# Merge and output projection of a hybrid decoder layer: block products with resident weights in place of a loop over groups with reloaded weights

## The chip, the cores and the metric

The kernel runs on one core of a Trainium2 chip. The metric is the device time of one execution in microseconds (us). Its engines run side by side, each through its own list of instructions in order: TensorE (PE) multiplies matrices, with its loads of the stationary operand shown apart as PEld; VectorE (DVE), ScalarE (ACT) and GpSimd (POOL) work on elements; SyncE (SP) issues the transfers between the memory on the chip and DRAM.

## The reference

The layer works on 2048 prompt tokens and on 32 sample tokens (8 sequences of 4). Three token mixers give `o_a` (512 channels, stick-breaking attention), `o_b` (512 channels, pooling) and `o_c` (1024 channels, gated linear attention). What the change touches is the end:

```
gates  = sigmoid(mg).reshape(B, T, 3, 1024)
merged = gates[:, :, 0] * (o_a @ w_pa) + gates[:, :, 1] * (o_b @ w_pb) + gates[:, :, 2] * (o_c @ w_pc)
y      = x + merged @ w_o
```

`w_pa` and `w_pb` are 512 x 1024, `w_pc` and `w_o` are 1024 x 1024. All inputs are float32, and the result is wanted in nearly that precision.

## The kernel before, in words

Every float32 matrix is held as two parts, hi (a rounded copy, cast by ACT) and lo (the rest, a subtraction on DVE or POOL). A product of two matrices then is three matmuls (hi x hi, hi x lo, lo x hi), issued by `mm3` (L114), 128 channels deep each. So whatever is multiplied first has to be cast and subtracted.

The program has three phases. Phase a (projections, attention, pooling) and phase b (gated linear attention) write the mixers' outputs to scratch in DRAM (`od`, 16 blocks of 128 channels for each of the 4 groups of 512 tokens; group 0 carries the 32 sample tokens as well and is 544 wide) and the gates (`gd`, 24 blocks). Phase c is the merge and the output projection. `phase_c` goes through the groups in the order 1, 2, 3, 0. For each one:

- it loads the 16 blocks of `od` as 8 tiles `oraw` (L1563), casts them on ACT (L1567) and subtracts on DVE (L1568);
- in each of 4 steps `dp` of 256 output channels it takes the weights of `w_pa`, `w_pb` and `w_pc`, multiplies (512 tokens wide, into PSUM banks `z`), applies the gates on DVE (L1597, L1600, L1602) and adds the branches on POOL (L1604); ACT and POOL split the merged block into `mh` and `ml` (L1607, L1608);
- in each of 4 more steps it takes the weights of `w_o` and multiplies with tokens stationary and 256 weight columns moving, into banks `pj`; DVE adds `x` (L1625), and the result is stored (L1626). For group 0 the sample tokens follow (L254, L255, L1632, L1633).

The weights come through `take`: raw tiles `wr` are loaded some steps ahead (L157), cast on ACT (L173) and subtracted on DVE and POOL in turn (L175). All 12 MB of weights go through that once for each of the 4 groups. The order of instructions on each engine is set at build time by a scheduler that puts later work forward where its own costs say that it fits; the chip then follows it to the letter. So phase c's first loads and casts stand inside the end of phase b, whose last steps are the normalisation of the last head (L1405, L283 to L288, L1414), eight transposes (L119), two copies `ocT` (L1447) and their stores to `od` (L1452).

Of the kernel before, what the change touches and what calls it, by code (L numbers as in the profile page):

```python
# [17 lines left out]
P = 128  # L18
# [58 lines left out]
def hybrid_step(ctx, tc, x_prompt, x_sample, cache_k, cache_v, state_pool, state_gla, page_table, norm_g, w_in,  # L77
# [21 lines left out]
    wp = ctx.enter_context(tc.tile_pool(name="wp", bufs=1))  # L99
# [122 lines left out]
    def plan_c(g):  # L222
        us = []
        for d0 in range(0, D, 256):
            us += [[(wpa[:, :, d0:d0 + 256], 256)], [(wpb[:, :, d0:d0 + 256], 256)]] + halves(wpc, [(d0, 256)])
        for d0 in range(0, D, 256):
            us += halves(wo, [(d0, 256)])
        return [(seg, "s", "gv") for seg in us]

# [67 lines left out]
    od = [[dtile([P, ncols(g)], f"od{g}_{k}") for k in range(16)] for g in range(NG)]  # L297
    gd = [[dtile([P, ncols(g)], f"gd{g}_{k}") for k in range(24)] for g in range(NG)]
# [6 lines left out]
    hp = ctx.enter_context(tc.tile_pool(name="hp", bufs=1))  # L305
# [9 lines left out]
    def phase_a(ctx):  # L315
# [298 lines left out]
        def v_step(st):  # L614
# [10 lines left out]
            if c == 0 and pr == 1:  # L625
                h = hd_.h
                if h % 2 == 0:
                    hd_.pair[0] = ap_.tile([P, TG], F32, name="oT", bufs=OTB)
                oT = hd_.pair[0]
                r = slice(64 * (h % 2), 64 * (h % 2) + 64)  # L630
                ro = slice(64 - 64 * (h % 2), 128 - 64 * (h % 2))
                nc.scalar.copy(oT[r], hd_.acc[ro])
                nc.vector.tensor_tensor(oT[r], oT[r], hd_.acc[r], op=add)
                nc.gpsimd.tensor_tensor(oT[r], oT[r], hd_.sg[r, :TG], op=mul)
                if h % 2 == 1:
                    nc.sync.dma_start(od[g][h // 2][:, :TG], oT)
# [57 lines left out]
        def pool_group(g, p, hT):  # L694
# [72 lines left out]
            nc.sync.dma_start(od[g][4 + p], ob[:, :n])  # L767
# [8 lines left out]
        def gate_unit(g, u, hT):  # L776
# [3 lines left out]
            for j, c0, m in ([(j, *sp) for sp in spans for j in range(2)] if u == gates_a(g) - 1 else  # L780
# [6 lines left out]
                if c0 + m == ncols(g):  # L787
                    nc.sync.dma_start(gd[g][u * 2 + j], gts[j][:, :ncols(g)])

        def gate_last(g, hT):  # L790
# [4 lines left out]
            for c0 in range(0, TG, 256):  # L795
                for u, w, gt in zip(us, ws, gts):
                    for j in range(2):
# [5 lines left out]
                        if c0:  # L803
                            nc.sync.dma_start(gd[g][u * 2 + j], gt[j][:, :TG])
# [110 lines left out]
    def sample_attn(ctx, cst):  # L915
# [67 lines left out]
        for bt in range(2):  # L983
# [68 lines left out]
            for c in range(4):  # L1052
                nc.sync.dma_start(od[0][c][:, TG + bt * 16:TG + (bt + 1) * 16], og[:, c, :])


    def phase_b(ctx):
# [157 lines left out]
        def proj_gate(g, hh, hT):  # L1214
            w = win_unit([(OFF_MG + (8 + hh) * 256, 256)])
            for j in range(2):
# [3 lines left out]
                nc.sync.dma_start(gd[g][(8 + hh) * 2 + j], gt[:, :ncols(g)])  # L1220

        def mix_head(g, hh, st, later=None):
# [218 lines left out]
            def finish():  # L1441
                for j in range(2):
# [9 lines left out]
                    nc.sync.dma_start(od[g][8 + hh * 2 + j], oT[:, :n])  # L1452
# [90 lines left out]
    def phase_c(ctx):  # L1543
        mq = ctx.enter_context(tc.tile_pool(name="mrq", bufs=1, reuse_waits="tile"))
        on = ctx.enter_context(tc.tile_pool(name="on", bufs=1, reuse_waits="tile"))
        mp = ctx.enter_context(tc.tile_pool(name="mrg", bufs=1, reuse_waits="tile"))
        oe = ctx.enter_context(tc.tile_pool(name="oe", bufs=1, reuse_waits="tile"))
        o1 = ctx.enter_context(tc.tile_pool(name="o1", bufs=1, reuse_waits="tile"))
        N = TG + TS

        def o_tiles(gi, k2):
            if k2 < 4 and gi % 2:
                return [HT[x][:, k2 * 2:k2 * 2 + 2, :] for x in range(2)]
            return [(on if k2 > 1 else o1).tile([P, 2, N], F32R, name=f"o{x}{k2}") for x in "hl"]

        for gi, g in enumerate((1, 2, 3, 0)):
            n = ncols(g)
            cols = ((0, 256), (256, 288)) if g == 0 else ((0, TG),)
            oh, ol = [], []
            for k2 in range(8):  # L1560
                raw = oe.tile([P, 2, N], F32, name="oraw", bufs=3)
                for i in range(2):
                    nc.sync.dma_start(raw[:, i, :n], od[g][k2 * 2 + i])  # L1563
                th, tl = o_tiles(gi, k2)
                oh.append(th)
                ol.append(tl)
                nc.scalar.copy(oh[k2][:, :, :n], raw[:, :, :n])  # L1567
                nc.vector.tensor_tensor(ol[k2][:, :, :n], raw[:, :, :n], f32(oh[k2])[:, :, :n], op=sub)  # L1568
            mh = mq.tile([P, NC, TG], F32R, name="mh")
            ml = mq.tile([P, NC, TG], F32R, name="ml")  # L1570
            mS = mq.tile([P, NC, 2 * TS], F32R, name="mS")
            for dp in range(4):
                d0 = dp * 256
                ms = [mp.tile([P, N], F32, name="m", bufs=2) for _ in range(2)]
                for br in range(3):
                    gts = []
                    for j in range(2):
                        gt = mp.tile([P, N], F32, name="gt", bufs=4)
                        nc.sync.dma_start(gt[:, :n], gd[g][br * 8 + dp * 2 + j])
                        gts.append(gt)  # L1580
                    if br < 2:
                        src = (wpa, wpb)[br]
                        wh, wl = take([(src[:, :, d0:d0 + 256], 256)])
                        wsl = [(wh[0][:, c], wl[0][:, c], br * 4 + c) for c in range(4)]
                    else:
                        wh, wl = take(*halves(wpc, [(d0, 256)]))
                        wsl = [(wh[c // 4][:, c % 4], wl[c // 4][:, c % 4], 8 + c) for c in range(8)]
                    for j in range(2):
                        js = slice(j * P, (j + 1) * P)
                        for c0, m in cols:  # L1590
                            cs = slice(c0, c0 + m)
                            ps = bank("z")
                            drain(mm3(ps[:, :m], [((a[:, js], b_[:, js]),
                                                   (oh[k // 2][:, k % 2, cs], ol[k // 2][:, k % 2, cs]))
                                                  for a, b_, k in wsl]))
                            if br == 0:
                                nc.vector.tensor_tensor(ms[j][:, cs], ps[:, :m], gts[j][:, cs], op=mul)  # L1597
                            else:
                                if br == 1:
                                    nc.vector.tensor_tensor(gts[j][:, cs], ps[:, :m], gts[j][:, cs], op=mul)  # L1600
                                else:
                                    nc.vector.scalar_tensor_tensor(gts[j][:, cs], gts[j][:, cs], 1.0, ps[:, :m],  # L1602
                                                                   op0=add, op1=mul)
                                nc.gpsimd.tensor_tensor(ms[j][:, cs], ms[j][:, cs], gts[j][:, cs], op=add)  # L1604
                for j in range(2):
                    c = dp * 2 + j
                    nc.scalar.copy(mh[:, c, :], ms[j][:, :TG])  # L1607
                    nc.gpsimd.tensor_tensor(ml[:, c, :], ms[j][:, :TG], f32(mh)[:, c, :], op=sub)  # L1608
                    if g == 0:
                        nc.scalar.copy(mS[:, c, :TS], ms[j][:, TG:])  # L1610
                        nc.gpsimd.tensor_tensor(mS[:, c, TS:], ms[j][:, TG:], f32(mS)[:, c, :TS], op=sub)
            for dp in range(4):
                d0 = dp * 256
                w = take(*halves(wo, [(d0, 256)]))
                pss = [bank("pj") for _ in range(2)]
                for cs in ((0, 6), (6, NC)) if dp == 0 else ((0, NC),):
                    for i in range(4):
                        proj_part(w, (mh, ml), i * P, P, pss[i // 2][:, i % 2 * 256:(i % 2 + 1) * 256], *cs,
                                  i % 2 == 0 or dp > 0)
                for pr in range(2):  # L1620
                    ps = pss[pr]
                    t0 = g * TG + pr * 256
                    xt = mq.tile([P, 2, 256], F32, name="xt", bufs=2)
                    nc.sync.dma_start(xt, xp[t0:t0 + 256, d0:d0 + 256].rearrange("(i p) n -> p i n", p=P))
                    nc.vector.tensor_tensor(xt, xt, ps.rearrange("p (i n) -> p i n", n=256), op=add)  # L1625
                    nc.sync.dma_start(yp[t0:t0 + 256, d0:d0 + 256].rearrange("(i p) n -> p i n", p=P), xt)  # L1626
                if g == 0:
                    xy = mq.tile([P, 2, 256], F32, name="xt", bufs=2)[:TS]
                    xt, yt = xy[:, 0], xy[:, 1]
                    nc.sync.dma_start(xt, xs[:, d0:d0 + 256])  # L1630
                    drain(proj_smp(w, mS, yt))
                    nc.vector.tensor_tensor(xt, xt, yt, op=add)  # L1632
# [53 lines left out]
```

## Time and profile before

| | |
|---|---|
| time, median of 3 runs | 3106.36 us (3098.63 to 3110.66) |
| the profiled execution: time / span | 3105.42 us / 3103.7 us |
| mean granted TensorE clock | 0.985 of full speed |
| share of the span that is busy: PE, DVE, ACT, POOL | 96%, 59%, 41%, 38% |
| traffic to and from DRAM over the span | 202 GB/s |
| phase c: first matmul to last instruction | 2540.99 to 3103.7 us |

The span runs from the first to the last instruction; the execution's own time lies 1.7 us above it. A granted clock of 1.00 is 2.4 GHz, half of it 1.2 GHz. Busy shares are means over a program of very different stages, so for a change in phase c the rows of phase c count.

### The profile page before, as it was taken

How to read it: one execution, taken by the hardware profiler on the slowest of the kernel's cores; microseconds unless marked ns; L12 is line 12 of the kernel's file. 1: busy time of each engine (PE TensorE's matmuls, PEld its weight loads, DVE VectorE, ACT ScalarE, POOL GpSimd, SP SyncE). 2: the span in 40 equal slices, each digit the busy share in tenths (PEclk: the TensorE clock that was granted, in tenths of full speed). 3: DMA queues.
4: the chain of work that ended last, by engine and by line, in shares of the span. 5: the costliest groups of instructions: out<-in, count | busy, mean ns of one | idle time of the engine just before them, and what ended most of it. 6: DMA issues, size and time to landing. Idle time of an engine off the chain costs nothing.

```text
span 3103.7 us, 55924 instructions
## 1 busy us (share of the span) xinstructions
PE 2983.7 (96%) x21874; PEld 2628.6 (85%) x21874; DVE 1843.9 (59%) x3776; ACT 1284.5 (41%) x2411; POOL 1183.4 (38%) x1161
## 2 busy tenths in 40 slices
PE   7999999999999999999989999999999989999999
PEld 7889987789878888777779988888778778988999
DVE  7776455656766778888745655545455564343332
ACT  2333334453554545665644433334334443232221
POOL 4556232314232434332224333333434436344452
PEclk9999999999999999999999999999999989999999
DMA  8867764556645764445565676564464456766553
GB/s 290 285 228 249 290 219 169 193 204 236 213 170 202 243 239 144 155 144 171 174 216 200 230 247 222 178 221 175 158 215 166 170 175 212 226 207 190 175 160 111
DMA packets 303037, 626.24 MB, mean 202 GB/s; under 512 B 26353, under 2 KB 188493, under 8 KB 265645
## 3 DMA queue, kind: packets, MB, share of 16 engines
q1 hardware_dynamic: 297652, 605.87, 57.7%
q0 software_dynamic: 5120, 16.78, 1.7%
q8 instruction: 173, 2.83, 0.4%
q14 instruction: 92, 0.75, 0.1%
HBM read 452.47 MB, written 170.28 MB: 201 GB/s over the span
## 4 chain that ended last, share of the span: by engine, by line
PE 42%; DVE 5%; ACT 3%; DMA 2%; issue 1%; SPq 1%; POOL 0%; ACTq 0%; DVEq 0%; POOLq 0%
PE pj L114 24%; PE z L114 13%; PE at L114 2%; PE acc L114 1%; DMA hTl<-hd 1%; PE z L119 1%; PE at L119 1%; DVE lv L1117 0%; PE acc L119 0%; DVE lv L1120 0%; DVE gate L1414 0%; DVE scx L1359 0%; ACT L1148 0%; DMA oraw<-od 0%; ACT lv L1119 0%
## 5 line engine op out<-in xcount | busy, mean ns | idle before, releaser
L114 PE MATMUL pj<-hTh,w 128*128 128x512 f32 (+2 forms) x3648 | 1055.8, 355 | 7.2 <-DVE ut L758 5.3
L114 PEld LDWEIGHTS pj<-hTh,w 128*128 128x128 f32 x3648 | 645.1, 189 | 111.9 <-issue 27.5
L114 PE MATMUL pj<-w,hTh 128*128 128x256 f32 (+1 forms) x3680 | 707.2, 292 | 13.0 <-DMA hTh<-hd 6.8
L114 PE MATMUL pj<-hTl,w 128*128 128x512 f32 (+2 forms) x1824 | 632.0, 346 | 0.0
L114 PEld LDWEIGHTS pj<-w,hTh 128*128 128x128 f32 (+1 forms) x3680 | 576.3, 191 | 31.2 <-issue 9.6
L114 PE MATMUL pj<-w,hTl 128*128 128x256 f32 (+1 forms) x1840 | 526.1, 286 | 7.9 <-DVE hTl L422 4.1
L585 POOL TENSOR_TENSOR be<-be,om 128x512 f32<-128x512 f32 (+1 forms) x160 | 167.8, 1049 | 556.4 <-DVE om L580 518.6
L114 PEld LDWEIGHTS pj<-hTl,w 128*128 128x128 f32 x1824 | 345.7, 190 | 26.7 <-issue 1.2
L175 POOL TENSOR_TENSOR w<-wr,w 128x1024 fp32r<-128x1024 f32 x104 | 255.6, 2458 | 284.5 <-ACT w L173 174.5
L114 PEld LDWEIGHTS pj<-w,hTl 128*128 128x128 f32 (+1 forms) x1840 | 352.7, 192 | 9.3 <-DVE hTl L422 4.5
L580 DVE TENSOR_TENSOR_SCAN om<-om,car 128x512 f32<-128x512 f32 x192 | 267.2, 1393 | 80.6 <-ACT om L572 80.4
L571 ACT ACTIVATE be<-z,bB 128x512 f32<-128x512 f32 (+2 forms) x320 | 200.3, 626 | 212.1 <-DVE z L568 136.8
L611 ACT CAST ah<-at 128x512 fp32r<-128x512 f32 (+2 forms) x352 | 160.8, 493 | 259.3 <-PE at L119 190.4
L612 DVE TENSOR_TENSOR al<-at,ah 128x512 fp32r<-128x512 f32 (+2 forms) x352 | 188.8, 563 | 118.5 <-ACT ah L611 117.7
L114 PE MATMUL z<-oh,w 128*128 128x512 f32 (+2 forms) x896 | 251.1, 365 | 0.0
L173 ACT CAST w<-wr 128x1024 fp32r<-128x1024 f32 x122 | 128.0, 1049 | 256.3 <-PE z L114 126.5
L572 ACT ACTIVATE om<-z,nbB 128x512 f32<-128x512 f32 (+2 forms) x320 | 200.4, 626 | 0.0
L114 PEld LDWEIGHTS z<-oh,w 128*128 128x128 f32 x896 | 161.4, 189 | 28.8
L114 PE MATMUL pj<-w,mh 128*128 128x256 f32 x1024 | 184.5, 283 | 0.6 <-ACT mh L1607 0.6
L119 PE MATMUL at<-ident,be 128*128 128x128 f32 x1088 | 148.0, 274 | 16.4 <-DVE qT L519 9.0
L114 PE MATMUL z<-ol,w 128*128 128x512 f32 (+2 forms) x448 | 163.6, 366 | 0.0
L114 PEld LDWEIGHTS pj<-w,mh 128*128 128x128 f32 x1024 | 159.6, 192 | 1.1 <-ACT mh L1607 0.8
(509 smaller groups left out, 5291.4 us busy)
## 6 DMA issues: line engine op xcount, KB each, us to landing
w<-wk SPq DMA_DIRECT2D x216, 1024.0 KB
wk<-w SPq DMA_DIRECT2D x72, 1024.0 KB
wr<-in_w_in_dram SPq DMA_DIRECT2D x56, 512.0 KB
gt<-gd SPq DMA_DIRECT2D x72, 256.0 KB
wr<-in_w_pc_dram SPq DMA_DIRECT2D x32, 512.0 KB
wr<-in_w_o_dram SPq DMA_DIRECT2D x32, 512.0 KB
gd<-gt SPq DMA_DIRECT2D x62, 256.0 KB
x<-in_x_prompt_dram SPq DMA_DIRECT2D x26, 512.0 KB
```

Of the source, the lines that this page charges most:

```text
L114: i = nc.tensor.matmul(*a, **k)
L119: i = nc.tensor.transpose(*a, **k)
L173: nc.scalar.copy(wh, raw)
L175: (nc.vector if el[count[0] % len(el)] == "v" else nc.gpsimd).tensor_tensor(wl, raw, f32(wh), op=sub)
L571: nc.scalar.activation(be[:, :w], z[:, :w], AF.Sigmoid, bias=bB[:, h:h + 1], scale=0.125)
L572: nc.scalar.activation(om[:, :w], z[:, :w], AF.Sigmoid, bias=nbB[:, h:h + 1], scale=-0.125)
L580: nc.vector.tensor_tensor_scan(ov, ov, ov, init, op0=mul, op1=ALU.min)
L585: (nc.vector if i % 2 == 0 else nc.gpsimd).tensor_tensor(be[:, :w], be[:, :w], om[:, 1:w + 1], op=mul)
L611: nc.scalar.copy(ah[:, jr, tr_], pv[:, jr, tr_])
L612: nc.vector.tensor_tensor(al[:, jr, tr_], pv[:, jr, tr_], f32(ah)[:, jr, tr_], op=sub)
```

## The change

Phase c is written anew as three stages, each of which goes through all groups with one set of weights, loaded and split once.

Stage 1 is the two small branches, plain: units of (group, branch) for the groups 1, 2, 0, 3, with `w_pa` and `w_pb` resident as 8 tiles `opw`. Each unit is as many matmuls as before, of the same shapes. The gated sum of the two goes to DRAM (`md[0]`).

Stage 2 is the third branch for the groups 0 to 3, as a Strassen-Winograd product: both matrices are cut into 2 x 2 blocks, and sums and differences of blocks are formed so that 7 block products do in place of 8. `left` and `right` form these operands on DVE (4 adds of 1024 columns for a group, and 4 for each half of the weights). The 7 weight operands are 14 tiles, resident for all groups. The products accumulate in three chains of PSUM banks (`PROD`: x, y, x, z, x, z, x). The adds that put the quadrants together, the gate, and the sum from `md[0]` are on DVE (`branch_evict`); the result goes to `md[1]`. Tokens are 256 wide (272 in group 0) where they were 512 (256 and 288).

Stage 3 is the output projection for the groups 1, 2, 3, 0 in the same way, with weights 512 columns wide as the moving side, where they were 256. The operands of `w_o` are formed during the last group of stage 2. The sample tokens take 32 matmuls beside the last group.

POOL keeps 7 of the weights' subtractions; all other work of that kind is DVE's. The pools of phases a and b are closed ahead of phase c (`front.close()`), and `od` and `gd` become one DRAM tile for each group. The rest of the diff in phases a and b follows from this, and the order of their instructions is nearly the one of before. The core of the diff:

```diff
-        for gi, g in enumerate((1, 2, 3, 0)):
...
-                for br in range(3):
...
-                        wh, wl = take(*halves(wpc, [(d0, 256)]))
...
-                w = take(*halves(wo, [(d0, 256)]))
...
+        def split(hi, lo, raw, eng=nc.vector):
+            nc.scalar.copy(hi, raw)
+            eng.tensor_tensor(lo, raw, f32(hi), op=sub)
+
+        def left(load, new, put):
+            a11 = load(0, 0)
+            yield put(a11)
+            a12 = load(0, 1)
+            yield put(a12)
+            a21, a22 = load(1, 0), load(1, 1)
+            s1, w = new()
+            nc.vector.tensor_tensor(s1, a21, a22, op=add)
+            nc.vector.tensor_tensor(a21, a11, a21, op=sub)
+            nc.vector.tensor_tensor(a11, s1, a11, op=sub)
+            yield put(a11)
+            yield put(s1)
+            yield put(a21)
+            nc.vector.tensor_tensor(a12, a12, a11, op=sub)
+            yield put(a12)
+            yield put(a22)
...
+        def put_w(raw):
+            t = ww.tile([P, 2, 2, TG], F32R, name="opw", bufs=14)
+            turn[0] += 1
+            split(t[:, 0], t[:, 1], raw, nc.gpsimd if turn[0] % 2 and turn[0] <= 14 else nc.vector)
+            return t
...
+        def product(ch, start, ws, acts, branch):
+            w = ch.w
+            ks = [(kp, kk) for kp in range(len(ws)) for kk in range(2)]
+            for m in range(4 if branch else 2):
...
+                    for x, y in ((0, 0), (0, 1), (1, 0)):
+                        n += 1
+                        mm(out, lhsT=L[x], rhs=R[y], start=start and m % ch.per == 0 and n == 1,
...
+        def run(dst, acts, w, branch, evict, each=None):
+            chains = {}
+            for i, kind in enumerate(PROD):
+                while len(dst[i]) < dst.need:
+                    go(1)
+                a = acts(i)
+                if i in (0, 1, 3):
+                    chains[kind] = Chain("x" if kind == "x" else "z", w)
+                product(chains[kind], i in (0, 1, 3), dst[i], a, branch)
+                evict(i, chains[kind])
...
+        def branch_evict(g):
...
+                gt = tile_g()[:, :, :w]
+                nc.sync.dma_start(gt, gd[g][:, 16 + fi * 4:16 + fi * 4 + 4, cs])
+                m = tile_g()[:, :, :w]
+                nc.sync.dma_start(m, md[0][g][:, rows, cs])
...
+                    for ps, sb in ch.parts(v):
+                        nc.vector.tensor_tensor(sb, ps, sb, op=add)
+                    nc.vector.scalar_tensor_tensor(v, gt, 1.0, v, op0=add, op1=mul)
...
+                nc.vector.tensor_tensor(v, v, m, op=add)
+                nc.sync.dma_start(md[1][g][:, rows, cs], v)
...
+            units = [(g, br) for g in (1, 2, 0, 3) for br in range(2)]
...
+        acts = feed([operand(od[g], 8, 4, ncols(g) // 2, right) for g in range(NG)], 1)
+        for g in range(NG):
+            if g == NG - 1:
+                plan_w([weights(wo, 4, kp, right) for kp in range(2)], wq, two)
+            run(wc, acts, ncols(g) // 2, True, branch_evict(g), (lambda i: go(1)) if g in (0, NG - 1) else None)
+        ORD = (1, 2, 3, 0)
...
+        acts = feed([operand(md[1][g], 0, 4, 256, left) for g in ORD], 1)
```

Three places of the order show what moved. The first is ScalarE where phase c begins. Before, these were its rows (`oh` is the hi part of phase c's first operands, `w` of its first weights, `ocT` the last copy of phase b):

```order
L1567 CAST oh_29855<-oraw 128x2x512
L1369 CAST Sh<-S_22340 128x256
L1405 ACTIVATE junk,gss<-at 128x256
L1567 CAST oh_29862<-oraw 128x2x512
L173 CAST w_29917<-wr 128x1024
L1369 CAST Sh<-S_22340 128x256
L1405 ACTIVATE junk,gss<-at 128x256
L1184 ACTIVATE gate<-pj 128x512
L173 CAST w_29920<-wr 128x1024
L1405 ACTIVATE junk,gss<-at 128x256 x2
L1447 COPY ocT<-z 128x512 x2
```

Now the same place reads (lines from here on are those of the changed kernel; `opw` is a weight operand, `opa` an activation operand; L1399 is the former L1405, L1441 the former L1447):

```order
L1363 CAST Sh<-S_22196 128x256
L1399 ACTIVATE junk,gss<-at 128x256
L1178 ACTIVATE gate<-pj 128x512
L1399 ACTIVATE junk,gss<-at 128x256 x2
L1441 COPY ocT<-z 128x512 x2
L1553 CAST opw<-rw 128x1024 x5
L1553 CAST opa_29738<-ra_29736 128x2x512
L1553 CAST opa_29743<-ra_29741 128x2x512
```

Four casts of phase c stood ahead of the copies `ocT`; now none does, and five casts of weights stand between the copies and the first operand.

The second place is VectorE where stage 1 passes into stage 2 (L1799 applies a gate, L1803 adds the branches, L1554 is the subtraction of a split, L1580 to L1587 form operands):

```order
L1799 TENSOR_TENSOR gt_31009<-z,gt_31009 128x512
L1554 TENSOR_TENSOR opw<-rw,opw 128x1024
L1799 TENSOR_TENSOR gt_31009<-x,gt_31009 128x512
L1554 TENSOR_TENSOR opw<-rw,opw 128x1024
L1803 TENSOR_TENSOR gt_31009<-gt_31009,gt_30877 128x2x512
L1554 TENSOR_TENSOR opa<-ra,opa 128x544 x4
L1580 TENSOR_TENSOR ra<-ra 128x1088
```

Before, VectorE passed from the small branches into the third one with nothing between the gates but a weight's subtraction:

```order
L1600 TENSOR_TENSOR gt<-z,gt 128x512 x2
L1602 SCALAR_TENSOR_TENSOR gt<-gt,z 128x512
L175 TENSOR_TENSOR w_30217<-wr,w_30217 128x1024
L1602 SCALAR_TENSOR_TENSOR gt<-gt,z 128x512
L1597 TENSOR_TENSOR m<-z,gt 128x512 x2
```

The operands' subtractions now stand behind the last gate and the last add of stage 1 and behind two weight tiles.

The third place is VectorE where stage 2 passes into stage 3 (L1731 and L1732 are the last evictions of stage 2, L1563 to L1569 form the operands of stage 3's first group, L1840 and L1846 add to `x`):

```order
L1564 TENSOR_TENSOR ra<-ra 128x4x256
L1587 TENSOR_TENSOR rw<-rw 128x1024
L1554 TENSOR_TENSOR opw<-rw,opw 128x1024
L1840 TENSOR_TENSOR gt<-x,gt 128x512
L1554 TENSOR_TENSOR opw<-rw,opw 128x1024
L1840 TENSOR_TENSOR gt<-x,gt 128x512
L1732 TENSOR_TENSOR tmp<-tmp,gt 128x4x256
L1554 TENSOR_TENSOR opw<-rw,opw 128x1024
L1732 TENSOR_TENSOR gt<-gt 128x4x256
L1554 TENSOR_TENSOR opw<-rw,opw 128x1024
L1565 TENSOR_TENSOR ra<-ra 128x4x256
L1554 TENSOR_TENSOR opw<-rw,opw 128x1024
```

Before, where it passed from the merge into the projection, it stood so:

```order
L1602 SCALAR_TENSOR_TENSOR gt<-gt,z 128x512
L1568 TENSOR_TENSOR ol_31013<-oraw,oh_31012 128x2x512
L1568 TENSOR_TENSOR ol_31020<-oraw,oh_31019 128x2x512
L1568 TENSOR_TENSOR ol_32094<-oraw,oh_32093 128x2x512
L1568 TENSOR_TENSOR ol_32101<-oraw,oh_32100 128x2x512
L175 TENSOR_TENSOR w_30627<-wr,w_30627 128x1024
L1568 TENSOR_TENSOR ol_32108<-oraw,oh_32107 128x2x512
L1625 TENSOR_TENSOR xt<-xt,pj 128x512 x2
```

Then it prepared the next group's operands there; now five of the 14 weight tiles of `w_o` and the first operands of stage 3 stand between the evictions of both stages.

## Rows read from the trace of the kernel before

**Rows 1.** The page's part on busy time: us, share of the span, instructions.

```profile
PE 2983.7 (96%) x21874; PEld 2628.6 (85%) x21874; DVE 1843.9 (59%) x3776; ACT 1284.5 (41%) x2411; POOL 1183.4 (38%) x1161
```

**Rows 2.** Waits of PE in phase c, 2548 to 3100 us: total, times, longest.

```profile
PE pj L114 <- ACT mh L1607: 0.6, 1, 0.6
PE pj L114 <- POOL ml L1608: 0.4, 1, 0.4
```

**Rows 3.** The chain that ended last: start, us, engine, work, instructions.

```profile
2522.82 4.10 DMA oraw<-od
2538.83 2.50 PE z L119 x8
2541.33 90.82 PE z L114 x384
2632.16 46.07 PE pj L114 x384
...
2678.23 89.17 PE z L114 x384
...
3047.00 53.02 PE pj L114 x445
```

**Rows 4.** Stretches: us, busy time (instructions) of each engine, granted clock, DMA.

```profile
2530.00:2550.00 20.00, 14.07 (x62) 11.24 (x61) 13.75 (x27) 8.62 (x16) 3.59 (x2) 0.74 0.66 210
...
2700.00:2750.00 50.00, 50.00 (x217) 40.39 (x216) 15.37 (x19) 12.57 (x14) 28.98 (x19) 1.00 0.55 164
...
2900.00:2950.00 50.00, 50.00 (x402) 49.22 (x401) 18.71 (x17) 14.59 (x15) 16.26 (x8) 1.00 0.57 179
```

**Rows 5.** Timeline of ACT at the start of phase c: start, us, work [idle before].

```profile
2527.00 1.05 ACT L1567 CAST oh<-oraw 128x1024 fp32r<-128x1024 f32 x1 [2.67 <-DMA oraw<-od]
...
2540.52 0.59 ACT L1447 COPY ocT<-z 128x512 f32<-128x512 f32 x1 [5.82 <-PE z L119]
2541.37 0.59 ACT L1447 COPY ocT<-z 128x512 f32<-128x512 f32 x1 [0.27 <-PE z L119]
2541.85 2.94 ACT L1567 CAST oh<-oraw 128x1024 fp32r<-128x1024 f32 x3
```

**Rows 6.** Timeline of SP's issues there.

```profile
2522.16 10.04 SPq L1563 DMA_DIRECT2D oraw<-od  x10
...
2541.13 1.17 SPq L1452 DMA_DIRECT2D od<-ocT  x2
```

**Rows 7.** Timeline of PE there.

```profile
2538.83 2.50 PE L119 MATMUL z<-ident,gate 128*128 128x128 f32 x8 [4.71 <-DVE gate L1414]
2540.99 0.78 PE L114 MATMUL z<-oh,w 128*128 128x512 f32 x1
...
2542.84 0.63 PE L114 MATMUL z<-ol,w 128*128 128x512 f32 x1
2543.26 1.05 PE L114 MATMUL z<-oh,w 128*128 128x512 f32 x2
...
2544.55 0.82 PE L114 MATMUL z<-oh,w 128*128 128x512 f32 x2
```

**Rows 8.** DVE and ACT: groups by shape, phase c (busy us, mean ns).

```profile
L1602 DVE SCALAR_TENSOR_TENSOR gt<-gt,z 128x512 f32<-128x512 f32 x24 | 16.4, 684 | 53.3 <-PE z L114 53.3
...
L173 ACT CAST w<-wr 128x1024 fp32r<-128x1024 f32 x92 | 96.6, 1050 | 236.6 <-PE z L114 126.5 <-PE pj L114 95.2 <-DMA wr<-in_w_pa_dram 5.9
```

**Rows 9.** DVE's subtractions, whole run or phase c: min/median/max ns, first and last start.

```profile
L175 DVE TENSOR_TENSOR w<-wr,w x46: 1212/1226/2614, 2549.7 to 3073.6; 128x1024 fp32r<-128x1024 f32 x46
...
L1317 DVE TENSOR_TENSOR qsl<-qs,qsh x16: 665/688/740, 1664.4 to 2518.3; 128x512 fp32r<-128x512 f32 x16
```

**Rows 10.** The end: timeline, last matmuls and last store.

```profile
3098.02 1.99 PE L114 MATMUL pj<-w,mS 128*64 128x256 f32 x16
...
3101.32 0.34 SPq L1633 DMA_DIRECT2D out_dram<-xt  x1
```

**Rows 11.** Transfers from 2540 to 3104 us: GB/s in 40 slices, and the whole.

```profile
GB/s 256 321 297 198 141 191 188 331 246 192 217 180 137 188 151 168 266 305 171 245 202 186 133 185 177 158 176 197 179 227 92 199 127 186 161 62 115 158 96 65
DMA packets 87240, 105.30 MB, mean 187 GB/s; under 512 B 5024, under 2 KB 67744, under 8 KB 87200
```

More of the change, by code (lines that the diff above doesn't have):

```diff
@@ L1556, in phase_c @@
-        for gi, g in enumerate((1, 2, 3, 0)):
[L1557 to L1574, printed above, removed]
-                for br in range(3):
-                    gts = []
-                    for j in range(2):
[L1578 to L1584, printed above, removed]
-                    else:
-                        wh, wl = take(*halves(wpc, [(d0, 256)]))
[L1587 to L1613, printed above, removed]
-                w = take(*halves(wo, [(d0, 256)]))
[L1615 to L1632, printed above, removed]
-                    nc.sync.dma_start(ys[:, d0:d0 + 256], xt)
@@ new lines, in put_w, with weights, load @@
+        def put_w(raw):
[3 more added lines that the diff above has]
+            return t
+        def weights(src, half, kp, form):
+            def load(i, j):
+                k, f = (j, i) if form is left else (i, j)
+                raw = raw_w()
+                c = k * half + kp * 2
+                nc.sync.dma_start(raw, src[:, c:c + 2, f * TG:(f + 1) * TG])
+                return raw
+            return form(load, lambda: (raw_w(), 0), put_w)
@@ new lines, in operand, with view, load, put @@
+        def operand(src, c0, half, w, form):
+            def view():
+                return raw_a()[:, :half, :w]
+            def load(i, j):
+                k, t = (i, j) if form is right else (j, i)
+                raw = view()
+                c = c0 + k * half
+                nc.sync.dma_start(raw, src[:, c:c + half, t * w:(t + 1) * w])
+                return raw
+            def put(raw):
+                got = []
+                for kp in range(half // 2):
+                    t = op_.tile([P, 2, 2, HW], F32R, name="opa", bufs=4)
+                    split(t[:, 0, :, :w], t[:, 1, :, :w], raw[:, kp * 2:kp * 2 + 2, :])
+                    got.append(t)
+                return got
+            return form(load, lambda: (view(), 0), put)
@@ new lines, in phase_c, with go, plan_w, step @@
+        steps = []
+        def go(n):
+            for _ in range(n):
+                if steps:
+                    steps.pop(0)()
+        def plan_w(gens, dst, order):
+            for i, k in order:
+                def step(g=gens[k], d=dst[i]):
+                    d.append(next(g))
+                steps.append(step)
+        def run(dst, acts, w, branch, evict, each=None):
[8 more added lines that the diff above has]
+                evict(i, chains[kind])
+                if each is not None:
+                    each(i)
@@ new lines, in feed, with get, tile_t, tile_g @@
+        def feed(gens, depth):
+            it = (v for g in gens for v in g)
+            ahead_ = []
+            def get(_):
+                while len(ahead_) < depth + 1:
+                    v = next(it, None)
+                    if v is None:
+                        break
+                    ahead_.append(v)
+                return ahead_.pop(0)
+            return get
+        def tile_t():
+            return tt.tile([P, 4, HW], F32, name="tmp", bufs=3)
+        def tile_g():
+            return gg.tile([P, 4, HW], F32, name="gt", bufs=5)
```

241 lines of the change are left out of this document (210 added, 31 removed).

## The prediction

> **What bounds the kernel now.** I read the page's busy times first [rows 1]: PE has work in 96% of the span, the others far less, so I look for waits of PE in the part that changes. From 2548 us to the end it waited twice, for 1.0 us together [rows 2]. The chain that ended last [rows 3] says the same from behind: past 2541 us it consists of PE alone, stretch after stretch of matmuls. So phase c is bound by the number of its matmuls and their spacing, and what DVE, ACT, POOL and the transfers do there costs nothing as long as it comes in time.
>
> The spacing comes from stretches in which PE never stopped [rows 4]: 217 matmuls of 512 columns in 50 us are 0.2304 us each, and 402 of 256 and 288 columns in turn (272 in the mean) are 0.1244. In the chain [rows 3] 384 matmuls of 256 columns took 46.07 us, 0.1200 each. That is more than half of 0.2304, so two narrow matmuls cost 4% more than a wide one.
>
> **What goes.** Before, phase c has 1152 matmuls of 512 columns (265.4 us), 768 of 272 (95.5), 1536 of 256 (184.3) and 64 for the sample tokens (53.02 - 46.07, about 7, in the chain's last row): 552.6 us with 7.4 for the last term, of the 559 us from 2540.99 [rows 7] to 3100.0 [rows 10].
>
> Now stage 1 keeps half of the first two terms: 132.7 + 47.8 = 180.5 us. Stage 2 has 7/8 of the other half's products, at half the width and twice the number: 336 x 0.1244 + 1008 x 0.1200 = 162.8 us in place of 180.5. This is 17.7 less and not an eighth (22.6), since it goes from 512 columns to 256. Stage 3 has 672 + 32 matmuls of 512: 162.2 us in place of 191.7. This is 29.5 less, over an eighth, since it goes the other way. The sum is 505.5 us, **47.1 us less**, if PE is fed throughout.
>
> The Trainium skill (TensorE: Matmul & The Clock Gate, section Back-to-back issue gap) gives a spacing of columns / 2.4 GHz + 2.5 ns. By it, as an estimate, the sums would be 512.2 and 469.7 us, 42.5 less. The rows are 7 to 10% above it at both widths, and the rows decide.
>
> **What is lost where the stages begin.** Before, phase c had its first operands loaded from 2522.16 us on [rows 6] and two of them cast ahead of the copies `ocT` [rows 5], so its matmuls followed the last transposes without a pause [rows 7].
>
> *Start.* Now ACT passes from the last `ocT` copy (ends 2541.96 [rows 5]) into five casts of weights at 1.05 us [rows 8] and then the first operand's cast, another 1.05: 2548.3. On SP the operands' loads stand behind the two `od` stores, whose issue ended at 2542.3 [rows 6]. A load of this kind took 4.10 us in the chain [rows 3]: 2546.5 to 2547, just hidden behind the casts. The first matmul moves from 2540.99 to about 2548.5: **+7.5 us**. The half clock is paid in both cases: after an idle time of 4.71 us matmuls of 512 columns began 0.42 us apart (2542.84, 2543.26) until 2544.55 [rows 7], with 0.74 granted in that stretch [rows 4]. Bounds: 5 (the casts get ahead of the copies at their actual times) and 10 (the second lo part is late as well).
>
> *Stage 1 to 2.* The last two weight tiles of `w_pc` go into buffers of `w_pb` that PE reads until its last matmul. Their casts stand ahead of the operands' casts on ACT, and on DVE two weight subtractions, the last gate and the last add stand ahead of the operands' (second place of the order). From the last matmul: 1.23 + 0.69 + 1.23 + 1.23 + 0.69 = 5.1 us [rows 8, 9] to the first lo part, of which a few matmuls hi x hi cover half a microsecond: **+4.5 us**. Below, 1.7 if only ACT's casts count; above, 7 with a half-clock restart.
>
> *Stage 2 to 3.* During the last group DVE must also make the operands of `w_o`: 14 subtractions and 8 adds at 1.23 us [rows 9], 27 us on top of its own work. That is 14 subtractions of 512 columns at 0.69 [rows 9] (9.7), 4 adds at 1.23 (4.9), and evictions of 3 x (2 x 0.69 + 2 x 1.23) + 2 x 0.69 + 1.23 = 14.1 us by the rows of 512 columns from PSUM [rows 8], 28.7 us in all, against 336 x 0.1200 = 40.3 us of PE. So the other groups leave DVE 11 us, the last one is short by up to 15 less what passes its end. Along the third place of the order, from the end of stage 2's matmuls: 0.69, two subtractions of 0.69, three operations of 1.23 (5.8 us, when stage 3's first product of 24 x 0.2304 = 5.5 us is done); two adds to `x`, two L1732, two weight tiles and L1565 (14.6 us); another weight tile, two adds, L1569, the operand's lo part (19.1 us). PE wants the third product's operand at 11.1. That is 8 us of waiting if DVE was level with PE at the end of stage 2, and up to 17 if it lags by 9. I take 11, plus 1.8 for a restart at half clock (3.56 us at half speed [rows 7]): **+13 us**.
>
> *Between groups.* Group 0 takes all four x banks, so group 1 waits for its evictions: **+1**. Elsewhere in stage 3 DVE has 9.7 + 4.9 + 16 x 0.69 = 25.6 us of work for 38.7 us of PE.
>
> *End.* The last store is of 512 KB in place of 32 KB. After the last matmul an add of 0.69, an issue of about 0.4, and by the 4.10 us of a load of two tiles [rows 3] a landing: 5.2 us in place of the 3.7 from 3100.0 to 3103.7 [rows 10]: **+1.5** (0 to 3).
>
> POOL falls nearly silent, which costs nothing here: its adds and subtractions go to DVE and are in the sums above. The DVE prices are those of undisturbed instructions, 1.226 us the median and 2.614 the longest [rows 9]. The Trainium skill (SBUF - State Buffer, section SBUF: two separate sides) has a lock between a DVE operation with two inputs from the chip's memory and a POOL operation; the spread of these rows agrees. Transfers shrink from 105.30 MB in phase c at 187 GB/s in the mean [rows 11] to about 102 MB (tile sizes times their numbers), 220 GB/s in stages 1 and 2 by the times above, below the 331 of a single slice [rows 11].
>
> **The sum:** -47.1 + 7.5 + 4.5 + 13 + 1 + 1.5 = -19.6 us, span 3084.1. With the 1.7 us that the profiled time lies above its span this is **3086 us**, 0.65% below the median of 3106.36 (the profiled execution lies 0.9 us below that median). Half a per cent, 15.5 us, is about what a measurement of this kernel can tell from no change.
>
> **The rivals.** *PE stays fed.* If DVE runs ahead in stage 2 (11 us free in each group) the passage to stage 3 costs 3 us and the others their lower bounds: -47.1 + 5 + 1.7 + 3 = -37, 3068 us. For it: PE hardly waited before [rows 2], with more weights to split. Against it: the order of the third place is fixed, and its count has 8 us of waiting with DVE level.
>
> *Late gates.* In stage 2 the gate and the sum of stage 1 are loaded per quadrant, into five buffers which free up when an eviction is done or a store has landed; SP issues in order, so a store that waits for DVE holds back the loads behind it. A load takes about 4 us [rows 3], a product 5.8. If DVE waits 1 to 2 us at each of 16 quadrants and half of that reaches PE, and the start and passages reach their upper bounds, this is 12 to 30 us more: 3098 to 3116. For it: 16 issues of 512 KB per group with pieces of 1 KB; against: three buffered products of slack.
>
> *Half clock in stage 2, slower than before.* The same wait, if it stops PE in each quadrant: 16 waits of a whole load (4.1 us) and a restart at half speed after each (1.8 us) are 94 us: 3180. It decides from 2.3 us lost per quadrant, 36 in all, on: then the time passes 3122. For it: after 4.71 us of idling PE did run at half clock [rows 7]; against: a lateness of DVE must first use up 11 us of slack in each group. The Trainium skill (TensorE: Matmul & The Clock Gate, section Loop structure matters more than you think) warns of a long wait for a transfer between matmuls, after which they run cold; the trace agrees at this one place.
>
> **How the numbers follow.** Forecast, 3074 to 3098: 0.50; fed, 3060 to 3074: 0.18; late gates, 3098 to 3122: 0.22; half clock: 0.10. Faster by over 0.5% means below 3090.8: all of the fed case and three quarters of the forecast, 0.55. Within 0.5%: the rest of the forecast and the late gates but for their end, 0.33. Slower: 0.12. The range 3064 to 3112 leaves out the half clock and the ends of both others.
>
> **What would show it.** Each step right: spacings of 0.230, 0.124 and 0.120 us in stretches without pause; PE's first matmul of phase c near 2548.5; one wait of 3 to 5 us where shapes change from 512 to 272 columns, one of 8 to 17 two products after the change from 256 to 512, with DVE's L1565 and L1569 named; few waits between. Wrong: waits of PE in every group with DVE held by a transfer (late gates), a granted clock below 0.95 over a whole stage (half clock), or no wait at the second passage (fed). A stage 2 whose matmuls are not 0.120 apart would break the first term itself.

## The result and the profile after

The changed kernel takes 3074.88 us (median of 5 runs, 3071.51 to 3086.17) where the kernel before took 3106.36 (3098.63 to 3110.66). The ratio is 0.9916, 95% interval 0.9902 to 0.9930: 0.84% faster. The profiled execution has a span of 3069.8 us, 33.9 less than before.

PE is as busy as before by its share; the page's line on busy time, which answers to [rows 1]:

```profile
PE 2935.0 (96%) x21362; PEld 2570.7 (84%) x21362; DVE 1992.2 (65%) x3968; ACT 1269.4 (41%) x2438; POOL 949.1 (31%) x1000
```

PE has 48.7 us less to do and DVE 148 more. PE's waits, from 2530 us on, are no longer the 1.0 us of phase c before [rows 2] (engine and line waiting, releaser, total, times, longest):

```profile
PE x L115 <- ACT opa L1553: 10.2, 2, 7.2
PE z L115 <- ACT opa L1553: 6.3, 1, 6.3
PE z L120 <- DVE gate L1408: 3.4, 1, 3.4
PE z L115 <- DVE opa L1554: 1.6, 1, 1.6
```

Every long one is a passage: 6.3 and 1.6 us where stage 1 begins, 3.0 and 7.2 (the 10.2) where stages 2 and 3 begin. The 3.4 belongs to phase b. Within the stages PE does not stop. In the chain that ended last, products of one shape take the same time one after the other (start, us, work, instructions; the first is a product of stage 2's first group with 272 columns, then one with 256, then one of stage 3 with 512):

```profile
2737.41 5.97 PE z L115 x48
...
2829.37 5.60 PE z L115 x48
...
2929.11 5.60 PE z L115 x24
```

So 272 columns cost 0.1244 us, 256 columns 0.1167 and 512 columns 0.2333. Whole stretches, which answer to [rows 4], say the same (us, busy time and instructions of PE, PEld, DVE, ACT, POOL, clock, DMA):

```profile
2550.00:2600.00 50.00, 50.00 (x217) 40.43 (x216) 38.19 (x38) 10.01 (x10) 8.75 (x3) 1.00 0.73 241
...
2790.00:2840.00 50.00, 50.00 (x431) 50.00 (x430) 30.07 (x38) 15.47 (x28) 0.00 (x0) 1.00 0.70 220
2940.00:2990.00 50.00, 50.00 (x216) 40.24 (x215) 30.30 (x42) 11.18 (x18) 0.00 (x0) 1.00 0.50 167
```

*The start.* PE's timeline, which answers to [rows 7], and ACT's, which answers to [rows 5]:

```profile
2530.49 2.50 PE L120 MATMUL z<-ident,gate 128*128 128x128 f32 x8 [3.40 <-DVE gate L1408]
2539.34 0.79 PE L115 MATMUL z<-opa,opw 128*128 128x512 f32 x1 [6.35 <-ACT opa L1553]
...
2542.49 0.63 PE L115 MATMUL x<-opa,opw 128*128 128x512 f32 x1
2544.73 1.65 PE L115 MATMUL z<-opa,opw 128*128 128x512 f32 x6 [1.61 <-DVE opa L1554]
```

```profile
2533.02 0.58 ACT L1441 COPY ocT<-z 128x512 f32<-128x512 f32 x1 [0.27 <-PE z L120]
2533.51 4.83 ACT L1553 CAST opw<-rw 128x1024 fp32r<-128x1024 f32 x5
2538.24 1.04 ACT L1553 CAST opa<-ra 128x1024 fp32r<-128x1024 f32 x1
2539.57 1.05 ACT L1553 CAST opa<-ra 128x1024 fp32r<-128x1024 f32 x1 [0.29 <-DMA ra<-od]
```

The five casts and the first operand's stand between `ocT` and the first matmul, as counted. From the last transposes to the first matmul it is 8.85 us where it was 2.16 [rows 7]. But the transposes themselves come at 2530.49, 8.3 us sooner than before; the experiments look at that.

*Stage 1 to 2*, on PE, ACT and DVE:

```profile
2722.13 2.96 PE L115 MATMUL x<-opa,opw 128*128 128x512 f32 x12
2728.07 1.28 PE L115 MATMUL x<-opa,opw 128*128 128x272 f32 x4 [2.99 <-ACT opa L1553]
2729.59 7.82 PE L115 MATMUL x<-opa,opw 128*128 128x272 f32 x44 [0.25 <-DVE opa L1554]
```

```profile
2725.12 1.04 ACT L1553 CAST opw<-rw 128x1024 fp32r<-128x1024 f32 x1 [0.34 <-PE x L115]
2727.37 1.19 ACT L1553 CAST opa<-ra 128x544 fp32r<-128x544 f32 x2 [1.21 <-DMA ra<-od]
```

```profile
2726.55 1.22 DVE L1554 TENSOR_TENSOR opw<-rw,opw 128x1024 fp32r<-128x1024 f32 x1
2727.68 1.22 DVE L1803 TENSOR_TENSOR gt<-gt,gt 128x1024 f32<-128x1024 f32 x1
2728.82 2.63 DVE L1554 TENSOR_TENSOR opa<-ra,opa 128x544 fp32r<-128x544 f32 x4
```

ACT is held by the load of the operand (`DMA ra<-od`), and DVE comes to the operand's lo part at 2728.82, nearly at the same time. In SP's order the load stands behind stage 1's stores, and these wait for DVE's adds L1803 (6.3 us in three waits between 2715 and 2730 us); it was issued as soon as they were, and whether it could have gone sooner was not tried:

```profile
2717.84 4.04 SPq L1804 DMA_DIRECT2D md<-gt  x2
2722.22 2.73 SPq L1614 DMA_DIRECT2D ra<-od  x4
```

After the pause 44 matmuls take 7.82 us by PE's row where 0.1244 each would make 5.5; the granted clock was 0.58 from 2730 to 2735 us and 1.00 again in the 5 us after that.

*Stage 2 to 3*, on PE, DVE and ACT (L1565 and L1569 form operands):

```profile
2891.10 3.87 PE L115 MATMUL x<-opw,opa 128*128 128x512 f32 x16
...
2897.59 4.77 PE L115 MATMUL z<-opw,opa 128*128 128x512 f32 x20
2909.57 2.08 PE L115 MATMUL x<-opw,opa 128*128 128x512 f32 x4 [7.21 <-ACT opa L1553]
2911.44 1.91 PE L115 MATMUL z<-opw,opa 128*128 128x512 f32 x4
2913.14 5.70 PE L115 MATMUL x<-opw,opa 128*128 128x512 f32 x20
```

```profile
2895.48 0.68 DVE L1731 SCALAR_TENSOR_TENSOR gt<-gt,x 128x512 f32<-128x512 f32 x1
...
2907.56 1.22 DVE L1565 TENSOR_TENSOR ra<-ra 128x1024 f32<-128x1024 f32 x1
...
2911.03 1.22 DVE L1569 TENSOR_TENSOR ra<-ra 128x1024 f32<-128x1024 f32 x1
2912.16 2.50 DVE L1554 TENSOR_TENSOR opa<-ra,opa 128x512 fp32r<-128x512 f32 x4
```

```profile
2908.89 2.18 ACT L1553 CAST opa<-ra 128x512 fp32r<-128x512 f32 x4 [8.16 <-DVE ra L1565]
```

The third product starts 18.5 us after the first of stage 3. (The L1731 shown is the last read of stage 2's PSUM banks.) Four matmuls behind the pause take 1.87 us (2909.57 to 2911.44), 0.47 each: half the rate, and the granted clock was 0.50 from 2910 to 2915 us. The 28 matmuls up to 2918.68 take 9.1 us where 0.2333 each would make 6.5.

*The end*, which answers to [rows 10]: the last matmul ends at 3065.3, the span 4.5 us later (3.7 before). Of the 33.9 us, then, 8.3 lie ahead of the last transposes and 25.6 behind them.

### The profile page after: what moved, and what is told of

Same layout as the page of the kernel before. It is cut to its first block, busy times and chain, and to the rows that moved or that the text cites. A ratio compares the mean times of both kernels' runs of the same rounds, so it can differ in the third digit from the quotient of the medians.

```text
span 3069.8 us, 54591 instructions
## 1 busy us (share of the span) xinstructions
PE 2935.0 (96%) x21362; PEld 2570.7 (84%) x21362; DVE 1992.2 (65%) x3968; ACT 1269.4 (41%) x2438; POOL 949.1 (31%) x1000
## 4 chain that ended last, share of the span: by engine, by line
PE 42%; DVE 5%; ACT 3%; DMA 2%; issue 1%; POOL 0%; SPq 0%; ACTq 0%; DVEq 0%; POOLq 0%
PE pj L115 19%; PE x L115 9%; PE z L115 9%; PE at L115 2%; PE acc L115 1%; DMA hTl<-hd 1%; PE z L120 1%; PE at L120 1%; DVE lv L1111 0%; PE acc L120 0%; DVE lv L1114 0%; DVE scx L1353 0%; ACT L1142 0%; DVE gate L1408 0%; ACT lv L1113 0%
## 5 line engine op out<-in xcount | busy, mean ns | idle before, releaser
L1553 ACT CAST opa<-ra 128x512 fp32r<-128x512 f32 (+3 forms) x128 | 86.0, 679 | 292.4 <-PE x L115 188.8
L115 PE MATMUL x<-opa,opw 128*128 128x256 f32 (+3 forms) x1248 | 197.2, 313 | 3.2 <-ACT opa L1553 3.0
L115 PEld LDWEIGHTS x<-opa,opw 128*128 128x128 f32 x1248 | 175.5, 191 | 17.0 <-ACT opa L1553 3.4
L176 POOL TENSOR_TENSOR w<-wr,w 128x1024 fp32r<-128x1024 f32 x56 | 137.8, 2460 | 143.1 <-DVE w L172 50.0
L115 PE MATMUL z<-opa,opw 128*128 128x256 f32 (+2 forms) x1056 | 168.6, 313 | 8.0 <-ACT opa L1553 6.3
L115 PEld LDWEIGHTS z<-opa,opw 128*128 128x128 f32 x1056 | 148.0, 189 | 22.0 <-ACT opa L1553 6.7
L120 PEld LDWEIGHTS at<-ident,be 128*128 128x128 f32 x1088 | 127.1, 141 | 34.0 <-ACT kX L521 9.8
```

The lines of the kernel that those rows point to most:

```text
L115: i = nc.tensor.matmul(*a, **k)
L120: i = nc.tensor.transpose(*a, **k)
L176: (nc.vector if el[count[0] % len(el)] == "v" else nc.gpsimd).tensor_tensor(wl, raw, f32(wh), op=sub)
L1553: nc.scalar.copy(hi, raw)
```

## The experiments

Phases a and b run some us early or late from one execution to the next, and chips differ (the kernel before took 3096 to 3097 us beside the experiments). So the table gives what the profile of one execution of each kernel shows from fixed points on, in us: from the last transposes of phase b to the end of the span, to the first matmul of phase c, and from the first matmul of stage 2 to that of stage 3 and on to the last of all.

| kernel | transposes to end | to first matmul | stage 2 | stage 3 |
|---|---|---|---|---|
| before | 564.9 | 2.2 | | |
| before_again | 563.4 | | | |
| changed | 539.3 | 8.85 | 163.0 | 174.2 |
| eighth_product | 582.6 | 9.1 | 186.9 | 194.0 |
| wo_half_on_pool | 544.0 | 8.85 | 170.0 | 170.8 |
| first_operands_early | 533.9 | 6.0 | 163.8 | 173.0 |
| last_wpc_on_pool | 539.6 | 8.9 | 163.4 | 173.6 |
| wo_formed_in_stage1 | 533.8 | 8.85 | 163.3 | 168.6 |
| both_passages | 529.4 | 6.0 | 164.1 | 168.6 |

**Does PE pace stages 2 and 3?**

```diff
                 product(chains[kind], i in (0, 1, 3), dst[i], a, branch)
+                if i == 2:
+                    product(chains[kind], False, dst[i], a, branch)
```

> This kernel repeats the third of the seven block products in every group of stages 2 and 3 (same operands, added once more into the same chain), so each group has eight products' matmuls with the operands and adds of seven; the repeated product is not part of the result. Theory (stages 2 and 3 are bound by PE, whose matmuls lie 5.60 us per product in the changed kernel's chain): eight products more, four of 5.6 and one of 5.97 less 5.6 us, that is 45 us, less what the longer groups give back at the passage from stage 2 to 3 (up to 9 us): 36 to 45 us longer from the first matmul of stage 2 to the last of stage 3. Rival (DVE or transfers pace these stages, and matmuls fill gaps): under 20 us longer.

Stage 2 took 23.8 us more (0.9 of it are four matmuls of stage 3 that stand in it) and stage 3 19.8 (its waits at the start fell from 7.2 to 5.6 us), 43.6 together. PE's rows: the first matmul of stage 2, the first after its last, the end.

```profile
2733.09 1.27 PE L115 MATMUL x<-opa,opw 128*128 128x272 f32 x4 [2.72 <-ACT opa L1553]
...
2919.96 2.96 PE L115 MATMUL x<-opw,opa 128*128 128x512 f32 x12
...
3110.02 3.90 PE L115 MATMUL x<-opw,opa 128*128 128x512 f32 x16
```

So PE paces both stages, and an eighth of the products is worth 44 us. From the transposes on this kernel takes 582.6 us where the kernel before took 564.9 and 563.4: resident weights and the new order, with the matmuls of eight products and the other work of seven, are 18 to 19 us slower than before (one execution of each, whole: 3120.11 and 3096.23 us on the same chip). Without the missing products there is no gain.

**The wait at stage 3: take work off DVE by giving it to POOL.**

```diff
-            ... nc.gpsimd if turn[0] % 2 and turn[0] <= 14 else nc.vector)
+            ... nc.gpsimd if turn[0] % 2 and (turn[0] <= 14 or turn[0] > 22) else nc.vector)
```

> The subtractions of every second weight tile of w_o go from DVE to POOL, 7 of 14 in the last group of stage 2. Theory (the 7.2 us wait of PE at the third product of stage 3 comes from DVE's booked-out last group): 7 x 1.22 = 8.5 us less work on DVE, so the wait and the 2 us of half clock behind it go, 6 to 9 us in the time from stage 2's first matmul to stage 3's last. Rival (POOL slows DVE's subtractions to 2.4 to 2.9 us while it runs, as at the start of phase c): the wait stays above 4 us or PE waits earlier in that group, gain under 3 us.

Stage 3 became 3.3 us shorter, but stage 2 7.0 longer: 3.6 us lost. The rival was right: PE now waited in the last group of stage 2, and longest for a lo part in stage 3's second product:

```profile
2911.40 7.27 PE L115 MATMUL z<-opw,opa 128*128 128x512 f32 x20 [4.81 <-DVE opa L1554]
```

DVE's groups by shape from 2850 to 2900 us (busy us, mean ns), first in the changed kernel, then here:

```profile
L1554 DVE TENSOR_TENSOR opa<-ra,opa 128x512 fp32r<-128x512 f32 x16 | 10.3, 680 | 0.0
...
L1587 DVE TENSOR_TENSOR rw<-rw 128x1024 f32<-128x1024 f32 x2 | 2.4, 1216 | 0.0
```

```profile
L1554 DVE TENSOR_TENSOR opa<-ra,opa 128x512 fp32r<-128x512 f32 x13 | 14.1, 1110 | 0.0
...
L1587 DVE TENSOR_TENSOR rw<-rw 128x1024 f32<-128x1024 f32 x1 | 3.4, 3421 | 0.0
```

The same subtraction takes 1.11 us in the mean instead of 0.68 while POOL, at 3.06 us per tile, subtracts beside it; DVE also waited 2.3 us for one of POOL's results. The Trainium skill (SBUF - State Buffer, section SBUF: two separate sides) tells of one lock for a DVE operation with two inputs from this memory and a POOL operation; these rows agree.

**The same wait: take work off DVE by doing it earlier.** The 8 adds for `w_o` move to stage 1, and their results go through DRAM.

```diff
+        def preform(src, half, kp, dst):
...
+            for k, raw in enumerate(right(load, lambda: (raw_w(), 0), lambda r: r)):
+                if k in (2, 3, 4, 6):
+                    nc.sync.dma_start(dst[k], raw)
...
+                    if u < 2 and mp == 3:
+                        preform(wo, 4, u, wod[u])
...
-                plan_w([weights(wo, 4, kp, right) for kp in range(2)], wq, two)
+                plan_w([formed(wo, 4, kp, wod[kp]) for kp in range(2)], wq, two)
```

> The 8 adds that form the operands of w_o run in stage 1's first two units, where DVE has time, and go through DRAM; the last group of stage 2 only loads and splits them. The order of DVE's rows keeps the operand L1565 behind two adds to x, but only one weight tile behind the end of stage 2. Theory (DVE's booked-out last group makes the 7.2 us wait at stage 3's third product): 8 x 1.22 = 9.8 us less there, the wait falls to 0 to 3 us and the restart at half clock with it, 5 to 9 us less from stage 2's first matmul to stage 3's last, with nothing on POOL that could slow DVE. Rival (the wait is for the first product's matmuls, whose evictions stand ahead of L1565 and L1569 in any case): 4 us or more of it stay.

Stage 3 fell from 174.2 to 168.6 us, stage 2 stayed. PE's wait at the third product:

```profile
2900.84 2.07 PE L115 MATMUL x<-opw,opa 128*128 128x512 f32 x4 [2.50 <-ACT opa L1553]
```

It is 2.5 us where it was 7.2. The restart at half rate behind it, which was expected to go, stayed (four matmuls in 1.87 us), but was over sooner: 28 matmuls take 8.1 us where they took 9.1. So DVE's booked-out last group was the cause of most of the wait. What is left of it was not taken apart; L1565 still stands behind the adds to `x` in DVE's order.

**The start.**

```diff
+                    raw = raw_w() if (g, br) == units[0] else ra.tile(...)
...
+            nxt = pairs(*units[0])
             wab = []
             for src in (wpa, wpb):
```

> The operands of stage 1's first unit are loaded into weight buffers that are free early, ahead of the weights, so their casts stand first behind the ocT copies on ACT, ahead of three weight casts where there were five. Theory (the start is set by the casts in line on ACT and by the loads behind the od stores): first matmul 2.5 to 3.5 us sooner after the last transposes begin, 5.5 to 6.3 us where it was 8.85. Rival (the lo parts from DVE and POOL, 2.4 to 2.9 us each while both run, set the pace): the first matmul comes sooner, but the wait for the first lo part grows by as much and the gain by the twentieth matmul is under 1 us.

```profile
2529.59 2.50 PE L120 MATMUL z<-ident,gate 128*128 128x128 f32 x8 [3.40 <-DVE gate L1408]
2535.61 1.22 PE L115 MATMUL z<-opa,opw 128*128 128x512 f32 x2 [3.51 <-ACT opw L1553]
```

The first matmul came 6.0 us after the transposes began, 2.8 sooner, and the wait of 1.6 us for the first lo part is gone as well. By the start of stage 2 the gain was 4.9 us. The casts in line on ACT and the late loads set the start; the run moves both at once and does not tell them apart.

**The passage from stage 1 to 2.**

```diff
-            ... nc.gpsimd if turn[0] % 2 and turn[0] <= 14 else nc.vector)
+            ... nc.gpsimd if turn[0] in (21, 22) or turn[0] % 2 and turn[0] <= 14 else nc.vector)
```

> The subtractions of the last two weight tiles of w_pc, which stand ahead of stage 2's first operands on DVE, go to POOL. Theory of the prediction (that line of work on DVE sets the passage from stage 1 to 2): the wait of 3.2 us shrinks by 2 to 2.5 us. Rival, read from the trace of the changed kernel (ACT's first cast of an operand waited 1.2 us for its load): the first matmul comes 3 us after the last one of stage 1 as before, and only the 0.25 us behind it go.

Nothing gained: PE waited 3.55 and 1.24 us. ACT and DVE there:

```profile
2719.99 1.19 ACT L1553 CAST opa<-ra 128x544 fp32r<-128x544 f32 x2 [1.77 <-DMA ra<-od]
```

```profile
2717.89 2.44 DVE L1803 TENSOR_TENSOR gt<-gt,gt 128x1024 f32<-128x1024 f32 x1
2720.66 4.38 DVE L1554 TENSOR_TENSOR opa<-ra,opa 128x544 fp32r<-128x544 f32 x4 [0.33 <-ACT opa L1553]
```

ACT waited for the load once more, and DVE's work, with POOL subtracting beside it, took 2.44 us for 1.22 and 4.38 for 2.63. The run shows that the load binds when the two subtractions are gone; what the passage costs with an earlier load was not tried.

**Why phase b ended sooner.**

```diff
-                ..., phases="abc"):
+                ..., phases="ab"):
```

> The kernel before, with phase c left out (no merge, no output projection), so that nothing of it stands in phase b. From the third to the last store of the state S (phase b's last head group) the kernel before took 141.2 us, the changed kernel and its four variants 135.4 to 136.9. Theory (the loads, casts and subtractions that the kernel before pulls into phase b's end cost it 4 to 5 us): 135 to 137.5 us here. Rival (the difference comes from closing the pools or from the DRAM tiles of the changed kernel): 140 to 142.

> The kernel before, unchanged, for the spread of its phases a and b between executions. Theory: the same interval of phase b takes 140 to 142 us again, while its start lies within 6 us of the first time. Rival (the 141.2 us was one disturbed execution): 135 to 138.

(The 141.2 us and the ranges named there are from the first of the four stores of `S` to the last, not from the third.) They were 133.6 us without phase c and 137.6 in the second execution of the kernel before. So the time without phase c lies beyond the first theory's range (135 to 137.5), on the side away from its rival, and the second theory fell by its own numbers: part of the 141.2 us was spread between executions. The piece in which the pulled-in work stands is the last one. SP's third and fourth store of `S` and PE's last transposes, in the kernel before, in its second execution, and without phase c:

```profile
2493.18 0.34 SPq L1408 DMA_DIRECT2D out_dram<-S  x1
2533.86 0.34 SPq L1408 DMA_DIRECT2D out_dram<-S  x1
```

```profile
2483.35 0.34 SPq L1408 DMA_DIRECT2D out_dram<-S  x1
...
2527.59 2.50 PE L119 MATMUL z<-ident,gate 128*128 128x128 f32 x8 [4.71 <-DVE gate L1414]
```

```profile
2484.81 0.34 SPq L1408 DMA_DIRECT2D out_dram<-S  x1
...
2525.51 2.50 PE L119 MATMUL z<-ident,gate 128*128 128x128 f32 x8 [3.40 <-DVE gate L1414]
```

From the third store to the transposes it is 45.65 us (to 2538.83 [rows 7]), 44.24 and 40.70. The changed kernel and the six with its phases a and b have 40.7 to 41.8 (the changed one 2489.62 to 2530.49). So the loads, casts and subtractions of phase c that stood in phase b's end [rows 5, 6] cost it 2.4 to 5.0 us, and that is what the changed kernel got back. One way shows in [rows 5]: ACT stood idle for 2.67 us until the load of phase c's first operand had landed, with a cast and the normalisation of phase b (L1369, L1405) in line behind. Of the 8.3 us, 4.8 lie in this piece and 3.6 ahead of the third store, where the two kernels' work is nearly the same; those are most likely the spread between executions, since the first store of `S` came between 2380.8 and 2394.4 us in the ten profiled executions.

**Both repairs together.**

> The changed kernel with first_operands_early and wo_formed_in_stage1 together. Theory: the gains add, 5 us at the start and 5 to 9 at the passage to stage 3, so 1.1 to 1.3% below the kernel before where the changed kernel is 0.84% below, about 10 to 14 us below the changed kernel. Rival (the preforming in stage 1's first units lies on DVE where the first operands' lo parts are made, and on SP ahead of loads): gain at the start lost, 5 us or less.

3060.19 us (median of 5 runs), ratio to the kernel before 0.9886, interval 0.9865 to 0.9906. From the transposes on it has 529.4 us, 9.9 less than the changed kernel, where 5.4 and 5.5 make 10.9. The gains add but for 1 us. By its time from the transposes on this is the fastest version here; the ratio's interval still touches that of the changed kernel (0.9902 to 0.9930).

## Why the prediction was right, point by point

**The frame held**: PE bound before and after, faster by less than the missing products, the rest paid at three passages. 3074.9 us lies in the range, but only at the lower edge of the forecast's own band (3074 to 3098). Forecast was 19.6 us less; the span shows 33.9 and the ratio 26 (0.84% of 3106). Of the 14 us by which the span fell further, 8.3 lie ahead of the last transposes, where the sum had nothing, and 6.0 in phase c. The sizes, term by term:

- *Missing products, -47.1.* They were worth 49.9 us. The step "two narrow matmuls cost 4% more than a wide one" failed: it took the 0.1200 us of the projection's matmuls for those of stage 2, which measured 0.1167, half of 0.2333. By the prediction's own sign (a stage 2 not 0.120 apart) this breaks the term. And 0.2304 was 1% too low, since a window also counts the matmuls cut by its edges; the chain's 89.17 us for 384 [rows 3] would have given 0.2322. In the changed kernel the two errors cancel, which is luck: stages 2 and 3 have 7 x 5.97 + 21 x 5.60 = 159.4 and 28 x 5.60 + 32 x 0.233 = 164.2 us of matmuls, against 162.8 and 162.2, and with the 182.0 us of stage 1's pieces in the chain the sum is 505.6, against 505.5. In the kernel before nothing cancels: its chain's pieces without a pause make 3 x 89.17 + 96.4 + 3 x 46.07 + 53.4 = 555.5 us, against 552.6; that is where the 2.8 us come from by which the term was too small.
- *Start, +7.5.* It cost 6.7 us more than before from the transposes to the first matmul, and 1.6 for the first lo part: 8.3, within the bounds, by the mechanism named.
- *Stage 1 to 2, +4.5.* It cost 6.2 us: 3.2 of waiting and 3.0 in the slow matmuls behind it (the first product takes 9.2 us with its wait of 0.25, the later ones 5.97). The 4.5 had nothing for a restart at half clock; only the upper bound of 7 had it. The lo part was ready about 4.4 us after stage 1's last matmul (2725.1 to 2728.82 + 0.66), near the 5.1 of the count. But the step that put the passage on DVE and ACT's weight casts missed the load, which was late as well and binds by itself.
- *Stage 2 to 3, +13.* The place was exact and the mechanism right; it cost 10.0 us, the 174.2 of stage 3 less its 164.2 of matmuls: 7.2 of waiting and 2.6 at half clock, where the sum had 1.8. The forecast had the operand's lo part 19.1 + 3 = 22.1 us after the end of stage 2; it was ready after 21.7. (The recorded list names two weight tiles ahead of L1565; its 14.6 us have three in them, as the order does.) The lag of DVE was 4.4 us and not 3 (the last L1731 at 2895.48, PE through with stage 2 at 2891.1), but operations of 1.22 us started 1.13 us apart, which the count of 1.23 did not have. What the count had not used are eight matmuls hi x hi, which need ACT's cast alone: they began 18.5 us after the end of stage 2 and filled the last 3 us.
- *Between groups, +1*: no wait there. *End, +1.5*: 0.8.
- *Together*: -49.9 + 8.3 + 6.2 + 10.0 + 0.8 = -24.6 us, and the 1.0 us of waits that the kernel before had of its own [rows 2] makes the 25.6 that the traces show from the last transposes on.
- *What the sum left out*: phase b, taken as unchanged, gave back 2.4 to 5.0 us, because phase c's early work no longer stands in it; with the spread ahead of it, this is the larger part of what took the time to the lower edge of the band. The start's 6.7 us are thus in part an exchange.

**The rivals.** Late gates and half clock in every group did not come: PE has no wait inside stage 2, and the eighth product cost its full 22.9 us there (5.97 + 3 x 5.60 = 22.8). Half clock came, but only at the three passages; and the way of the late gates, a store that waits for DVE with loads in line behind it, is there once, where stage 1 passes into stage 2. The fed case was half true: stages fed throughout, passages not.

## What to carry to other kernels

When a matrix algorithm with fewer products makes the matmul engine faster, the gain is as sure as that engine's stretches are unbroken, and it is lost at the seams, where the first operands of the next stage wait behind the last work of the one before: count there, row by row in each engine's order, what stands ahead of the first operand. Work given to an idle engine can cost more than it takes away where the two slow each other (3.6 us lost here); doing it earlier on the same engine was the better repair (5.6 us won in stage 3). And work pulled ahead into another phase has a price in that phase, so its removal has a gain (2.4 to 5.0 us here).

## What the runs showed that was not expected

256-column matmuls ran at 0.1200 us in the projection before and at 0.1167 in stage 2, both without a pause and with a busy weight load; why, no run tells. What the half clock cost at stage 3's third product did not follow the length of the wait ahead of it. The 28 matmuls behind it, 6.5 us at 0.2333 each, took 9.1 after a wait of 7.2 us in the changed kernel, but 8.1 after one of 7.1 in first_operands_early (2904.32 to 2912.42). After waits of 2.5 us they took 8.14 in wo_formed_in_stage1 (2900.84 to 2908.98) and 8.19 in both_passages (2895.16 to 2903.35). In the first of these two the first four matmuls took 1.87 us, in the second 1.26, as the granted clock fell a little later there (0.73 from 2895 to 2897 us, 0.61 from 2897 to 2900).
